# A decoder layer with 32 experts: the final sums, the norm and the output of most tokens moved into the expert loop

## The chip, the cores and the metric

The kernel runs on one core of one Trainium2 chip. The metric is the device time of one execution in microseconds (us), the median of several runs. The engines are TensorE (PE in the profile, its weight loads PEld), VectorE (DVE), ScalarE (ACT), GpSimd (POOL) and SyncE (SP, which here only issues transfers). Each engine works through its own instructions in order and waits on semaphores for the others; a wait holds everything behind it on that engine.

## The reference

One layer on 1024 tokens of 1024 numbers, all float32. Attention comes first, then a mixture of experts:

```
x = x + g1 * sb_mixer(norm(x) * (1 + sc1) + sh1)         # stick-breaking attention, 16 heads
h = norm(x) * (1 + sc2) + sh2
grp = argmax(h @ w_grp + b_grp)                          # 1 of 4 groups of 8 experts
p, top2 = top_k(softmax(expert logits in that group), 2)
y = sum over the 2 experts of gate_e * (silu(h @ w_gate[e]) * (h @ w_up[e])) @ w_down[e]
out = rms_norm(x + g2 * y, final_g)                      # over the 1024 numbers of a token
```

Each token goes to two of the 32 experts, both in the same group. Its output needs both expert results.

## The kernel before

The first 700 us are projections, attention and routing. They leave in DRAM `x1_d` (x after attention) and `h2_d` (the input of the experts), and on the chip, for every expert, a list of its tokens.

The expert loop (from 700 to 1280 us) walks the 32 experts in order, 128 token slots each. A planner's list MU sets the order: four units `gu` (gate and up products, a quarter of the contraction each) of expert e, then two units `dn` (the down product) of expert e - 1. Each unit takes two weight tiles of 512 KB, which SP loads far ahead (as far as the free buffers allow, less a reserve of RM). Matmuls are done in three float32r products of a high and a low part, so every weight tile is split: ACT rounds it to `hi` (L124), DVE subtracts to get `lo` (L127). `m_split(n + SLEAD)` puts the split two units ahead of its use, so in the program ACT and DVE do unit n + 2 right after PE's matmuls of unit n.

Around the units, per expert: POOL gathers the tokens' rows `xg` by an indirect DMA (L1112); PE transposes them (L1140), ACT and DVE split them (`xTh` L1142, `xTl` L1143); after the gate and up products (PE, L1156, L1158, L1160) ACT does Silu and DVE the product `sg` (L1168, L1169); PE transposes `sg` (L1177), ACT and DVE split it (`hhl`, L1181, L1182); after the down product (PE, L1197) DVE multiplies by the gate and by g2 (`ys`, L1209), and POOL scatters `ys` to `y2_d` by an indirect DMA (L1119). `y2_d` has a row per token and choice.

In expert 2, `overflow_lists` counts on DVE whether an expert has more than 128 tokens (L1217 to L1240); PE gives it one small matmul (L1215).

After the loop comes a branch for such overflows (none is taken with these inputs), and then the tail: for each of 8 tiles of 128 tokens SP loads two rows of `y2_d` per token, DVE adds both to x1 (L1370, L1371), ACT sums the squares (L1373), POOL takes the power -1/2 (L1377), DVE scales (L1383), and ACT's queue writes the tile out (L1384).

## Time and profile before

| | us |
|---|---|
| median of 3 runs | 1331.52 (1331.03 to 1332.09) |
| the profiled execution | 1330.46 |
| its span, from the first to the last instruction | 1328.7 |
| PE busy in the span | 1225.2 (92%) |
| DVE busy | 1139.9 (86%) |
| ACT busy | 815.4 (61%) |
| POOL busy | 252.3 (19%) |
| expert loop, per expert (transposes of sg, 1243.3 to 1261.3) | 17.9 |
| from the end of the last matmul to the end of the span | 48.3 |

Busy shares are averages over the whole span. Matmuls overlap each other, and their ends are modelled, so a PE that is busy all the time may still be waiting for its inputs now and then; the start times of its instructions tell. An idle time in brackets is that of the engine before the instruction, with what ended it.

### The profile page before, as it was taken

Reading aid. Unit: us, or ns where it says so; the run is one execution under the profiler, and the core shown is the slowest. Engines: PE = TensorE matmul, PEld = TensorE weight load, DVE = VectorE, ACT = ScalarE, POOL = GpSimd, SP = SyncE. Lnnn points to the kernel's source line nnn. Section 1 sums busy time; section 2 is a strip of 40 time slices with the busy share of each in tenths; the row PEclk is TensorE's granted clock in tenths of the full one; section 3 lists DMA queues with packets and bytes.
Section 4 is the critical chain, followed back from the end, with each engine's and each line's share of the span. In section 5 each row is a group of like instructions: output and inputs, shape, how many; then the busy total and the mean of one; then the engine's idle time right before and its main releaser. Section 6 shows DMA issues by size and latency. Waiting matters only on the chain.

```text
span 1328.7 us, 19369 instructions
## 1 busy us (share of the span) xinstructions
PE 1225.2 (92%) x6788; PEld 983.1 (74%) x6788; DVE 1139.9 (86%) x1518; ACT 815.4 (61%) x1176; POOL 252.3 (19%) x329
## 2 busy tenths in 40 slices
PE   3999999999999999899979999999999999999950
PEld 3887777777777876578867788888888888888830
DVE  5868888988776859958788999999999999999957
ACT  6546455544556657732227778777777877777732
POOL 2502222211122213201211231111111111111101
PEclk9999999999999999999989999999999999999985
DMA  9311234333310212376428999999999999999467
GB/s 358 123 33 40 80 96 135 90 96 99 114 42 25 62 40 87 128 257 235 146 96 342 408 388 386 383 384 384 391 379 391 381 385 375 386 380 391 172 270 274
DMA packets 123395, 306.68 MB, mean 231 GB/s; under 512 B 16976, under 2 KB 49816, under 8 KB 123296
## 3 DMA queue, kind: packets, MB, share of 16 engines
q1 hardware_dynamic: 110256, 275.99, 56.4%
q0 software_dynamic: 11776, 25.20, 5.2%
q10 hardware_dynamic: 1264, 4.23, 0.8%
q8 instruction: 54, 0.88, 0.3%
q14 instruction: 45, 0.37, 0.1%
HBM read 288.58 MB, written 33.57 MB: 242 GB/s over the span
## 4 chain that ended last, share of the span: by engine, by line
issue 45%; PE 33%; DVE 9%; POOL 9%; DMA 2%; ACT 2%; POOLq 0%; SPq 0%; DVEq 0%; ACTq 0%
PE pm L115 6%; PE pm L117 5%; PE pm L116 5%; POOL y_d L1119 5%; PE pm L582 3%; PE z L513 3%; DVE S L540 3%; PE pm L555 3%; POOL xg L1112 2%; PE z L115 2%; PE z L117 2%; PE z L116 2%; DVE lo L127 1%; PE pm L718 1%; DVE p L541 1%
## 5 line engine op out<-in xcount | busy, mean ns | idle before, releaser
L127 DVE TENSOR_TENSOR lo<-wr,hi 128x1024 fp32r<-128x1024 f32 x384 | 447.3, 1221 | 11.5 <-ACT hi L124 7.4
L124 ACT CAST hi<-wr 128x1024 fp32r<-128x1024 f32 x384 | 380.4, 1050 | 17.1 <-PE pm L1197 7.2
L540 DVE TENSOR_TENSOR_SCAN S<-S 128x128 f32<-128x128 f32 (+3 forms) x192 | 186.4, 1012 | 23.1 <-POOL S L522 20.2
L1156 PE MATMUL z<-hi,xTh 128*128 128x512 f32 x512 | 162.2, 398 | 0.8 <-ACT xTh L1142 0.8
L1158 PE MATMUL z<-lo,xTh 128*128 128x512 f32 x512 | 160.3, 393 | 1.1 <-DVE lo L127 0.9
L1160 PE MATMUL z<-hi,xTl 128*128 128x512 f32 x512 | 158.9, 391 | 0.1
L1197 PE MATMUL pm<-hi,hhl 128*128 128x512 f32 x512 | 150.8, 397 | 0.0
L556 ACT COPY aT<-pm 128x512 f32<-128x512 f32 (+2 forms) x192 | 80.8, 493 | 69.3 <-PE pm L555 68.5
L1158 PEld LDWEIGHTS z<-lo,xTh 128*128 128x128 f32 x512 | 96.4, 188 | 23.9 <-DVE lo L127 2.7
L1160 PEld LDWEIGHTS z<-hi,xTl 128*128 128x128 f32 x512 | 96.2, 188 | 21.8 <-DVE xTl L1143 0.4
L520 POOL TENSOR_SCALAR_AFFINE_SELECT S<-S 128x256 f32<-128x256 f32 x64 | 51.1, 799 | 317.7 <-ACT S L516 310.7
L1156 PEld LDWEIGHTS z<-hi,xTh 128*128 128x128 f32 x512 | 93.9, 189 | 19.6 <-ACT xTh L1142 1.2
L1197 PEld LDWEIGHTS pm<-hi,hhl 128*128 128x128 f32 x512 | 94.1, 189 | 18.6
L115 PE MATMUL pm<-hTh,hi 128*128 128x512 f32 x256 | 107.1, 418 | 0.0
L541 DVE TENSOR_TENSOR p<-p,S 128x256 f32<-128x256 f32 (+3 forms) x96 | 92.5, 963 | 10.6 <-ACT p L517 2.0
L516 ACT ACTIVATE S<-z 128x256 f32<-128x256 f32 (+3 forms) x96 | 79.2, 825 | 34.6 <-PE z L513 18.0
L116 PE MATMUL pm<-hTl,hi 128*128 128x512 f32 x256 | 100.2, 392 | 0.0
L117 PE MATMUL pm<-hTh,lo 128*128 128x512 f32 x256 | 100.2, 391 | 0.0
L1119 POOL DMA_INDIRECT y_d<-ys,tbsi x32 | 64.2, 2007 | 188.4 <-DVE ys L1209 184.8
L1112 POOL DMA_INDIRECT xg<-h_d,tbgi x32 | 34.2, 1068 | 305.8 <-PE pm L1140 297.0
L517 ACT ACTIVATE p<-z 128x256 f32<-128x256 f32 (+3 forms) x96 | 78.5, 818 | 22.1 <-DVE acc L461 9.3
L555 PE MATMUL pm<-ident,p 128*128 128x128 f32 x576 | 79.8, 280 | 11.5 <-DVE v L397 6.0
(224 smaller groups left out, 2203.6 us busy)
## 6 DMA issues: line engine op xcount, KB each, us to landing
wr<-in_moe_w_gate_dram SPq DMA_DIRECT2D x128, 512.0 KB, 11.5
wr<-in_moe_w_up_dram SPq DMA_DIRECT2D x128, 512.0 KB, 11.3
wr<-in_moe_w_down_dram SPq DMA_DIRECT2D x128, 512.0 KB, 11.4
ad<-in_ada_w_dram SPq DMA_DIRECT2D x32, 512.0 KB, 4.0
ada<-in_ada_w_dram SPq DMA_DIRECT2D x16, 512.0 KB, 9.0
wq<-in_sb_w_in_dram SPq DMA_DIRECT2D x16, 512.0 KB, 5.1
x<-in_x_dram SPq DMA_DIRECT2D x8, 512.0 KB, 9.3
wv<-in_sb_w_in_dram SPq DMA_DIRECT2D x8, 512.0 KB, 5.4
```

Of the source, the lines that this page charges most:

```text
L115: nc.tensor.matmul(pt, lh, rh, start=start, stop=False)
L116: nc.tensor.matmul(pt, lh, rl, start=False, stop=False)
L117: nc.tensor.matmul(pt, ll, rh, start=False, stop=stop)
L124: nc.scalar.copy(hi, raw)
L127: (nc.vector if lo_eng == "v" else nc.gpsimd).tensor_tensor(lo, raw, hi, op=ALU.subtract)
L540: nc.vector.tensor_tensor_scan(r, r, r, s[:, h, n:n + 1], op0=ALU.mult, op1=ALU.bypass)
L555: nc.tensor.transpose(pt[:, j, :], p[:, h, j * P:(j + 1) * P], ident)
L1119: s = nc.gpsimd.indirect_dma_start(out=y2_d[:, :], out_offset=bass.IndirectOffsetOnAxis(ap=idx, axis=0), in_=ys[:, :], in_offset=None, bou ...
L1156: nc.tensor.matmul(gu[:, s, :], xh_[:, k, :], sp[s][0][:, k2, :], start=k == 0, stop=False)
L1158: nc.tensor.matmul(gu[:, s, :], xh_[:, k, :], sp[s][1][:, k2, :], start=False, stop=False)
L1160: nc.tensor.matmul(gu[:, s, :], xl_[:, k, :], sp[s][0][:, k2, :], start=False, stop=k == ND - 1)
L1197: nc.tensor.matmul(py[nh], a[:, f, :], sp[j][b][:, ns], start=f == 0 and a is hth and b == 0, stop=f == NF - 1 and a is htl)
```

## The change

Tokens are put in the order of the later one of their two experts. The first 128 tokens of that order are expected to be done after expert 8, the next after 12, and so on (`DONE`); seven of the eight tiles of 128 get their sum, norm and output inside the loop or right behind it, and the eighth after the branches.

- In routing, `r_gate` also keeps the later expert of each token (`later`).
- In expert 2, behind the overflow lists, `order_tokens` computes each token's place in that order: eight small additions in a row on DVE, three small matmuls on PE, and more DVE work. Then POOL writes the token numbers to `perm_d` by eight indirect DMAs of 128 numbers each, loads the list back as `permc`, and DVE makes `perm2` from it and tests on the chip whether the first seven tiles are really done at their experts (`bad`, counted into `ctl`).
- Two experts after `DONE`, POOL gathers the tile's rows of x1 and both of `y2_d`. One expert later DVE adds, scales by g2 and adds (`f_sum` in three steps, one behind each of the first three splits), ACT sums the squares, POOL takes the power, DVE scales, and POOL scatters the rows to the output.
- The product with g2 leaves `y_unit`: it becomes one ACT instruction per half with the gate as scale.
- `y2_d` is filled with zeros in the attention stage (four writes of 2 MB), because a tile is gathered while later experts are missing if the test fails.
- If the test fails, a second branch does the seven tiles once more. The reserve RM is 7 in place of 4.

The diff, cut to its core:

```
-RM = 4
+RM = 7
+DONE = (8, 12, 16, 20, 24, 28, 30)
...
+    perm_d = dram.tile([T, 1], I32, name="perm_d")
...
+        nc.vector.tensor_tensor(later[:, t:t + 1], ef[:, 0:1], ef[:, 1:2], op=ALU.max)
...
+            if hp == 5 and u in (0, 2, 4, 6):
+                if u == 0:
+                    yz = blk(nm="yz")
+                    nc.gpsimd.memset(yz, 0.0)
+                nc.sync.dma_start(y2_d[u * 256:u * 256 + 512, :].rearrange("(a p) d -> p a d", p=P),
+                                  yz[:, None, :].to_broadcast([P, 4, 1024]))
...
-            nc.vector.scalar_tensor_tensor(ys[:, ns], py[nh], gate[:, e:e + 1], g2r[:, ns], op0=ALU.mult, op1=ALU.mult)
+            nc.scalar.activation(ys[:, ns], py[nh], AF.Copy, scale=gate[:, e:e + 1])
...
+        bad, many = order_tokens(thr), small([P, 1], nm="many", bufs=1, pool=more)
+        nc.vector.tensor_reduce(many, bad, axis=AX, op=ALU.add)
+        nc.vector.tensor_tensor(ctl[:, 17:18], many, cum[:, 31:32], op=ALU.add)
...
+    def order_tokens(thr):
+        lastm = blk((P, NT, 32), BF16, nm="lastm")
+        nc.vector.tensor_tensor(lastm, io128[:, None, 0:32].to_broadcast([P, NT, 32]),
+                                later[:, :, None].to_broadcast([P, NT, 32]), op=ALU.is_equal)
+        lastc = blk((P, NT + 1, 32), BF16, nm="lastc")
+        nc.vector.memset(lastc[:, 0, :], 0.0)
+        for t in range(NT):
+            nc.vector.tensor_tensor(lastc[:, t + 1, :], lastc[:, t, :], lastm[:, t, :], op=ALU.add)
...
+        nc.tensor.matmul(pr[:, 0:256], tri, lastm.rearrange("p t e -> p (t e)"), start=True, stop=False)
+        nc.tensor.matmul(pr[:, 0:256], onesb, lastc[:, 0:NT, :].rearrange("p t e -> p (t e)"), start=False, stop=True)
+        nc.tensor.matmul(pc[:, 0:32], onesb, lastc[:, NT, :], start=True, stop=True)
...
+        nc.vector.tensor_copy(spi, spf)
+        ws = []
+        for t in range(NT):
+            w = nc.gpsimd.indirect_dma_start(out=perm_d[:, :],
+                                             out_offset=bass.IndirectOffsetOnAxis(ap=spi[:, t:t + 1], axis=0),
+                                             in_=tokc[:, t:t + 1], in_offset=None, bounds_check=T - 1,
+                                             oob_is_err=False)
...
+        nc.gpsimd.dma_start(permc, perm_d.rearrange("(s p) o -> p (s o)", p=P))
+        nc.vector.tensor_scalar(perm2, permc, float(T), None, op0=ALU.add)
+        bad = small([P, 7], nm="bad", bufs=1, pool=more)
+        nc.vector.tensor_tensor(bad[:, 0:6], cum[:, 8:29:4], thr[:, 0:6], op=ALU.is_lt)
+        nc.vector.tensor_tensor(bad[:, 6:7], cum[:, 30:31], thr[:, 6:7], op=ALU.is_lt)
...
+    def f_gather(s, c1, c2):
+        FX[s] += [blk(nm="fa"), blk(nm="fb")]
+        rows_of(FX[s][1], y2_d, c1, 2 * T)
+        rows_of(FX[s][2], y2_d, c2, 2 * T)
+
+    def f_sum(s, step):
+        fx, fa, fb = FX[s]
+        if step == 0:
+            nc.vector.tensor_tensor(fa, fa, fb, op=ALU.add)
+        elif step == 1:
+            nc.vector.tensor_tensor(fa, fa, g2r, op=ALU.mult)
+        else:
+            nc.vector.tensor_tensor(fx, fx, fa, op=ALU.add)
+            nc.scalar.activation(fb, fx, AF.Square, accum_out=ss)
+            nc.scalar.activation(ms, ss, AF.Identity, scale=1.0 / D, bias=epsc)
+            nc.gpsimd.tensor_tensor(rstd, ms, mhalf, op=ALU.pow)
+
+    def f_out(s, c1):
+        fx, rstd = FX.pop(s)
+        nc.vector.scalar_tensor_tensor(fx, fx, rstd, fgr, op0=ALU.mult, op1=ALU.mult)
+        nc.gpsimd.indirect_dma_start(out=out[0], out_offset=bass.IndirectOffsetOnAxis(ap=c1, axis=0),
+                                     in_=fx[:, :], in_offset=None, bounds_check=T - 1, oob_is_err=False)
...
             m_split(n + SLEAD)
+            for s_, d_ in enumerate(DONE[:6]):
+                if e == d_ + 2 and q == 0:
+                    f_rows(s_, col(permc, s_))
+                    f_gather(s_, col(permc, s_), col(perm2, s_))
+                if e == d_ + 3 and q < 3:
+                    f_sum(s_, q)
+            if e == E - 1 and q == 3:
+                for s_ in (6, 7):
+                    f_rows(s_, col(permc, s_))
...
             m_split(n + SLEAD)
             m_fill(RM, len(MU))
+            for s_, d_ in enumerate(DONE[:6]):
+                if e == d_ + 2 and q == 0:
+                    f_out(s_, col(permc, s_))
...
                 y_unit(e)
+                if e == DONE[6]:
+                    f_gather(6, col(permc, 6), col(perm2, 6))
+    for k in range(3):
+        f_sum(6, k)
+    f_out(6, col(permc, 6))
     nx = nc.values_load(ctl[0:1, 16:17], min_val=0, max_val=15)
+    again = nc.values_load(ctl[0:1, 17:18], min_val=0, max_val=32)
...
-    for t in range(4):
-        f_load(t)
-    for t in range(NT + 1):
-        if t < NT:
-            f_sum(t)
-            if t + 4 < NT:
-                f_load(t + 4)
-        if t > 0:
-            f_out(t - 1)
+    with tc.If(again > 0):
+        with tc.For_i(0, 7, 1) as j:
+...
+    f_gather(7, col(permc, 7), col(perm2, 7))
+    for k in range(3):
+        f_sum(7, k)
+    f_out(7, col(permc, 7))
```

What it moves on the engines is seen best in their instruction order. First DVE in expert 2, at the end of the overflow lists and the start of the splits for expert 3 (`ctl` holds the overflow counts, `wr` is a raw weight tile). Before:

```order
L1236 TENSOR_TENSOR xb_7644<-io_312,xb_7644 128x16 [waits DVE_49]
L1237 TENSOR_SCALAR xb_7644<-xb_7644 128x16 [waits DVE_49]
L1239 TENSOR_SCALAR ctl_7648<-xe_7641 128x16
L1240 CAST ctl_7648<-cum_7637 128x1
L127 TENSOR_TENSOR lo_7667<-wr_7238,hi_7666 128x1024 [waits DMAHW4_49,Activation_49]
L127 TENSOR_TENSOR lo_7671<-wr_7240,hi_7670 128x1024 [waits DMAHW5_49,Activation_49]
```

And in the changed kernel, whose line numbers are its own (`spi` are the places that POOL's eight writes go to, `permc` the list that it loads back):

```order
L1291 TENSOR_REDUCE spf_7688<-sp_7685 128x8 [waits DVE_49]
L1294 CAST spi_7690<-spf_7688 128x8 [waits DVE_49]
L1306 TENSOR_SCALAR perm_7117<-permc_7116 128x8 [waits DMASW7_49]
L1308 TENSOR_TENSOR bad_7718<-lcum_7682,thr_7641 128x6
L1309 TENSOR_TENSOR bad_7718<-lcum_7682,thr_7641 128x1
L1257 TENSOR_REDUCE many_7721<-bad_7718 128x1 [waits DVE_49]
L1258 TENSOR_TENSOR ctl_7658<-many_7721,cum_7647 128x1 [waits DVE_49]
L128 TENSOR_TENSOR lo_7740<-wr_7276,hi_7739 128x1024 [waits DMAHW0_49,Activation_49]
L128 TENSOR_TENSOR lo_7744<-wr_7278,hi_7743 128x1024 [waits DMAHW1_49,Activation_49]
```

The splits now stand behind an instruction that waits for a DMA of POOL's (DMASW7).

Second, ACT in an expert that carries a tile (expert 11, from its second `gu` unit on). Before:

```order
L1181 CAST hhl_9232<-pm_9227 128x512 [waits PE_49]
L124 CAST hi_9247<-wr_8859 128x1024 [waits DMAHW4_49,DVE_49]
L124 CAST hi_9251<-wr_8861 128x1024 [waits DMAHW5_49,DVE_49]
L124 CAST hi_9271<-wr_8891 128x1024 [waits DMAHW6_49,PE_49]
L124 CAST hi_9275<-wr_8893 128x1024 [waits DMAHW7_49,PE_49]
L1168 ACTIVATE sg_9283<-z_9178 128x512 [waits PE_49]
```

And in the changed kernel (`fx` is the tile's sum, which DVE's third step of `f_sum` writes):

```order
L1195 CAST hhl_9317<-pm_9312 128x512 [waits DVE_49,PE_49]
L125 CAST hi_9332<-wr_8990 128x1024 [waits DMAHW1_49]
L125 CAST hi_9336<-wr_8992 128x1024 [waits DMAHW2_49]
L1338 ACTIVATE fb_9097,ss_9341<-fx_9092 128x1024 [waits DMASW2_49,DVE_49]
L1340 ACTIVATE fms_9343<-ss_9341,epsc 128x1 [waits Activation_49]
L125 CAST hi_9367<-wr_9019 128x1024 [waits DMAHW3_49,PE_49]
L125 CAST hi_9371<-wr_9021 128x1024 [waits DMAHW4_49,PE_49]
L1182 ACTIVATE sg_9379<-z_9257 128x512 [waits PE_49]
```

Two casts of `hi` now stand behind a sum of squares that waits for DVE.

Third, POOL at the end of the loop. Before it has only the last scatters and the branch:

```order
L1119 DMA y_d<-ys_7651,tbsi_7105 2048x1024 [waits DMASW5_49,DVE_49]
L1119 DMA y_d<-ys_7444,tbsi_7105 2048x1024 [waits DMASW6_49,DVE_49]
L1119 DMA y_d<-ys_7651,tbsi_7105 2048x1024 [waits DMASW7_49,DVE_49]
L1294 TENSOR_LOAD ctl_7648 [waits DMAHW3_49,DMAHW2_49,DMAHW4_49,DMAHW1_49,DMAHW5_49,DMAHW0_49,DMAHW6_49,DVE_49,DMAHW7_49,Activation_49,Pool_49]
L1295 COMPARE_AND_BRANCH
```

And in the changed kernel:

```order
L1133 DMA y_d<-ys_7458,tbsi_7122 2048x1024 [waits Activation_49]
L1316 DMA fa_13169<-y_d,permc_7116 128x1024 [waits DMASW2_49,DMASW1_49,PE_49]
L1316 DMA fb_13170<-y_d,perm_7117 128x1024 [waits PE_49]
L1133 DMA y_d<-ys_7724,tbsi_7122 2048x1024 [waits DMASW3_49,DMASW2_49,Activation_49]
L1342 TENSOR_TENSOR frstd_13215<-fms_13213,mhalf 128x1 [waits Activation_49]
L1349 DMA out_dram<-fx_13099,permc_7116 1024x1024 [waits DMASW5_49,DMASW0_49,DVE_49]
L1419 TENSOR_LOAD ctl_7658 [waits DMAHW3_49,DMAHW2_49,DMAHW4_49,DMAHW1_49,DMAHW5_49,DMAHW0_49,DMAHW6_49,DVE_49,DMAHW7_49,Activation_49,Pool_49]
L1420 TENSOR_LOAD ctl_7658 [waits DVE_49]
L1421 COMPARE_AND_BRANCH
```

The gathers of tile 6 stand ahead of the last expert's scatter, which waits for both of them (DMASW2, DMASW3), and tile 6's output stands ahead of the branches.

## Rows read from the trace of the kernel before

**Rows 1.** Busy time by stretch; columns: stretch, length, engines, PE clock, DMA share, GB/s

```profile
700.00:704.00 4.00, 3.89 (x14) 3.34 (x15) 4.00 (x16) 2.49 (x4) 0.99 (x1) 0.56 0.32 111
705.00:770.00 65.00, 63.03 (x291) 50.72 (x291) 61.13 (x70) 48.34 (x56) 10.21 (x7) 1.00 1.02 406
850.00:1150.00 300.00, 300.00 (x1408) 249.12 (x1407) 294.19 (x302) 232.75 (x270) 45.04 (x33) 1.00 1.00 383
```

**Rows 2.** Waits for the split, 770 to 1250 us: who, for whom, total, times, longest

```profile
ACT hi L124 <- PE pm L1197: 7.2, 26, 0.3
DVE lo L127 <- ACT hi L124: 5.0, 24, 0.3
```

**Rows 3.** Timeline of DVE in expert 2: start, us, engine, line, operation

```profile
746.86 0.39 DVE L1222 TENSOR_TENSOR gtb<-cnts,thr 128x224 f32<-128x224 f32 x1
...
751.27 0.15 DVE L1240 CAST ctl<-cum 128x1 int32<-128x1 f32 x1
751.33 2.35 DVE L127 TENSOR_TENSOR lo<-wr,hi 128x1024 fp32r<-128x1024 f32 x2
```

**Rows 4.** Timeline of PE in expert 2

```profile
745.13 0.19 PE L1215 MATMUL pm<-macc,onesb 128*128 128x32 bf16 x1
...
752.60 0.49 PE L1158 MATMUL z<-lo,xTh 128*128 128x512 f32 x1 [0.25 <-DVE lo L127]
```

**Rows 5.** Timeline of POOL: the first and the third of three gathers issued in a row

```profile
695.73 1.10 POOL L1112 DMA_INDIRECT xg<-h_d,tbgi  x1 [5.62 <-DVE e L837]
...
698.46 1.34 POOL L1112 DMA_INDIRECT xg<-h_d,tbgi  x1 [0.30 <-issue]
```

**Rows 6.** The gathers of xg between 694 and 704 us (4 of them)

```profile
DMA to landing us min/median/max: 4.2/4.6/5.4
```

**Rows 7.** The gathers of xg between 770 and 1230 us (25 of them)

```profile
DMA to landing us min/median/max: 7.2/7.4/8.7
```

**Rows 8.** POOL's writes of x1_d (512 KB each, 600 to 700 us)

```profile
DMA to landing us min/median/max: 2.9/3.6/7.0
```

**Rows 9.** POOL's writes of mod_d (2 KB each)

```profile
DMA to landing us min/median/max: 1.6/1.8/6.2
```

**Rows 10.** Timeline of DVE in experts 29 and 30

```profile
1239.09 1.40 DVE L1209 SCALAR_TENSOR_TENSOR ys<-pm,tbl,g2r 128x512 f32<-128x512 f32 x2
1240.41 4.62 DVE L127 TENSOR_TENSOR lo<-wr,hi 128x1024 fp32r<-128x1024 f32 x4
```

**Rows 11.** Timeline of ACT there

```profile
1236.67 4.85 ACT L124 CAST hi<-wr 128x1024 fp32r<-128x1024 f32 x5
```

**Rows 12.** Timeline of PE there: readings of lo by three units, and the last matmuls

```profile
1253.46 0.63 PE L1197 MATMUL pm<-lo,hhl 128*128 128x512 f32 x2
...
1256.20 0.62 PE L1158 MATMUL z<-lo,xTh 128*128 128x512 f32 x2
...
1262.16 0.63 PE L1158 MATMUL z<-lo,xTh 128*128 128x512 f32 x2
...
1279.84 0.61 PE L1197 MATMUL pm<-hi,hhl 128*128 128x512 f32 x2
```

**Rows 13.** Timeline of DVE in the tail

```profile
1288.91 1.22 DVE L1370 TENSOR_TENSOR ya<-ya,x 128x1024 f32<-128x1024 f32 x1 [7.23 <-DMA ya<-y_d]
...
1295.43 1.28 DVE L1383 SCALAR_TENSOR_TENSOR x<-x,frstd,fgr 128x1024 f32<-128x1024 f32 x1 [0.47 <-POOL frstd L1377]
```

**Rows 14.** Timeline of ACT in the tail

```profile
1295.04 1.06 ACT L1373 ACTIVATE yb<-x 128x1024 f32<-128x1024 f32 x1 [0.72 <-DVE x L1371]
```

**Rows 15.** Timeline of POOL in the tail

```profile
1281.95 0.97 POOL L1119 DMA_INDIRECT y_d<-ys,tbsi  x1 [3.66 <-DVEq L1295]
...
1296.60 0.55 POOL L1377 TENSOR_TENSOR frstd<-fms,mhalf 128x1 f32<-128x1 f32 x1 [1.20 <-ACT fms L1375]
```

**Rows 16.** SP's first load, and ACT's last two writes, of the tail

```profile
1285.29 0.33 SPq L1363 DMA_DIRECT2D ya<-y_d  x1
...
1319.77 2.53 ACTq L1384 DMA_DIRECT2D out_dram<-x  x2
```

More of the change, by code (lines that the diff above doesn't have):

```diff
@@ L683, in decoder_layer @@
     mcum = [macc0]
+    later = const.tile([P, NT], F32, name="later")
     posall = const.tile([P, 2 * NT], F32, name="posall")
@@ L1237, in overflow_lists @@
         nc.vector.tensor_scalar(xb, xb, 1.0, float(P), op0=ALU.add, op1=ALU.mult)
-        ctl = small([P, 17], I32, nm="ctl", bufs=1, pool=more)
+        ctl = small([P, 18], I32, nm="ctl", bufs=1, pool=more)
         nc.vector.tensor_scalar(ctl[:, 0:16], xe, 31.0, None, op0=ALU.min)
@@ L1241, in overflow_lists @@
         free(gtb, le)
+        bad, many = order_tokens(thr), small([P, 1], nm="many", bufs=1, pool=more)
+        nc.vector.tensor_reduce(many, bad, axis=AX, op=ALU.add)
+        nc.vector.tensor_tensor(ctl[:, 17:18], many, cum[:, 31:32], op=ALU.add)
         return ctl, xb
+    permc = small([P, NT], I32, nm="permc", bufs=1, pool=more)
+    perm2 = small([P, NT], I32, nm="perm2", bufs=1, pool=more)
+    def order_tokens(thr):
[6 more added lines that the diff above has]
+            nc.vector.tensor_tensor(lastc[:, t + 1, :], lastc[:, t, :], lastm[:, t, :], op=ALU.add)
+        tokc = blk((P, NT), I32, nm="tokc")
+        nc.gpsimd.iota(tokc, pattern=[[P, NT]], base=0, channel_multiplier=1)
+        pr, pc = pm(), pm()
+        nc.tensor.matmul(pr[:, 0:256], tri, lastm.rearrange("p t e -> p (t e)"), start=True, stop=False)
+        nc.tensor.matmul(pr[:, 0:256], onesb, lastc[:, 0:NT, :].rearrange("p t e -> p (t e)"), start=False, stop=True)
+        nc.tensor.matmul(pc[:, 0:32], onesb, lastc[:, NT, :], start=True, stop=True)
+        tot = small([P, 32], nm="ltot", bufs=1, pool=more)
+        nc.vector.tensor_copy(tot, pc[:, 0:32])
+        cum = small([P, 32], nm="lcum", bufs=1, pool=more)
+        nc.vector.tensor_tensor_scan(cum, tot, tot, 0.0, op0=ALU.add, op1=ALU.bypass)
+        nc.vector.tensor_tensor(tot, cum, tot, op=ALU.subtract)
+        a = blk((P, NT, 32), nm="sp")
+        nc.vector.tensor_tensor(a, pr[:, 0:256].rearrange("p (t e) -> p t e", e=32),
+                                tot[:, None, :].to_broadcast([P, NT, 32]), op=ALU.add)
+        free(pr, pc)
+        nc.vector.tensor_tensor(a, a, lastm, op=ALU.mult)
+        spf = small([P, NT], nm="spf", bufs=1, pool=more)
+        nc.vector.tensor_reduce(spf, a, axis=AX, op=ALU.add)
+        free(a, lastm, lastc)
+        spi = small([P, NT], I32, nm="spi", bufs=1, pool=more)
+        nc.vector.tensor_copy(spi, spf)
[5 more added lines that the diff above has]
+                                             oob_is_err=False)
+            for o in ws:
+                tc.declare_no_dep(w.ins, o.ins, reason="each token has a place of its own")
+            ws.append(w)
+        free(tokc)
+        nc.gpsimd.dma_start(permc, perm_d.rearrange("(s p) o -> p (s o)", p=P))
[3 more added lines that the diff above has]
+        nc.vector.tensor_tensor(bad[:, 6:7], cum[:, 30:31], thr[:, 6:7], op=ALU.is_lt)
+        return bad
@@ new lines, in decoder_layer, with rows_of, f_rows @@
+    FX = {}
+    def rows_of(dst, src, idx, n):
+        nc.gpsimd.indirect_dma_start(out=dst[:, :], out_offset=None, in_=src[:, :],
+                                     in_offset=bass.IndirectOffsetOnAxis(ap=idx, axis=0),
+                                     bounds_check=n - 1, oob_is_err=False)
+    def f_rows(s, c1):
+        FX[s] = [blk(nm="fx")]
+        rows_of(FX[s][0], x1_d, c1, T)
+    def f_gather(s, c1, c2):
+        FX[s] += [blk(nm="fa"), blk(nm="fb")]
+        rows_of(FX[s][1], y2_d, c1, 2 * T)
+        rows_of(FX[s][2], y2_d, c2, 2 * T)
@@ new lines, in f_sum @@
+    def f_sum(s, step):
[6 more added lines that the diff above has]
+            nc.vector.tensor_tensor(fx, fx, fa, op=ALU.add)
+            ss = small([P, 1], nm="ss", bufs=3, pool=more)
+            nc.scalar.activation(fb, fx, AF.Square, accum_out=ss)
+            ms = small([P, 1], nm="fms", bufs=3, pool=more)
+            nc.scalar.activation(ms, ss, AF.Identity, scale=1.0 / D, bias=epsc)
+            rstd = small([P, 1], nm="frstd", bufs=3, pool=more)
+            nc.gpsimd.tensor_tensor(rstd, ms, mhalf, op=ALU.pow)
+            free(fa, fb)
+            FX[s] = (fx, rstd)
```

52 lines of the change are left out of this document (19 added, 33 removed).

## The prediction

> **What bounds the kernel now.** I read the busy times by stretch first, then the waits, then the timelines of the three places where the order changes. Between 850 and 1150 us PE is busy for 300.00 of 300 us at its full clock, DVE for 294.19, ACT for 232.75, and the DMA engines are at share 1.00 with 383 GB/s [rows 1]. A busy PE alone proves little, so the waits decide: no row there has PE waiting for anything, and no split waits for a load; the splits wait 7.2 us for PE and 5.0 us for ACT in 480 us [rows 2]. So PE's own pace bounds the loop, at 17.9 us an expert. DVE has about 2% in hand, which the departing `ys` widens by 1.40 us an expert [rows 10]. That removal cannot speed the loop up; what the change can win is in the tail, 48 us without a matmul, and it pays for that by what it puts into the loop.
>
> DVE's lead over PE is short. The program splits two units ahead, 6.0 us by PE's readings of `lo` at 1256.20 and 1262.16 [rows 12], and a unit's two splits take 2.3 of that (four in 4.62 [rows 10]). A DVE that stands still for longer than the rest stops PE.
>
> **Expert 2: the order of tokens.** Here lies the largest term. Today DVE ends the overflow lists at 751.42 and starts the splits for expert 3 at 751.33 [rows 3]; the first of them is what PE waits for at 752.60 [rows 4], so every later start there is PE's delay. Now between the two:
>
> - The test for equality (256 numbers, as the 0.39 us of 224 [rows 3], so 0.43), a small memset (0.15), eight additions at about 0.21 with their gaps (the small cast takes 0.15 [rows 3]): 753.7. PE's three small matmuls at 0.19 [rows 4] wait for that: 754.3. Copy, scan, subtraction, three passes over 256 numbers and a cast, 2.3: the places are ready at 756.6.
> - POOL issues eight indirect DMAs. Three in a row start 1.36 us apart [rows 5], so the eighth starts at 756.7 + 7 x 1.36 = 766.2. It lands 4.6 us later when the queues are nearly empty [rows 6], 7.4 when they are full [rows 7]. No buffer comes free while DVE stands, so loads cease: I take 4.6, 770.8.
> - POOL loads the list. Its plain writes land after 3.6 us [rows 8], so at 774.6. It can't be less than 1.6 (2 KB, [rows 9]).
> - DVE makes `perm2` and four small results, 5 x 0.21: 775.7.
>
> The splits start 24.4 us late. Of that PE can fill nothing: what it has in hand (two `dn` units, 6.6 us) it would have done anyway. The clock adds to it: around 700 us, after short waits, PE ran at 0.56 of its clock for 4 us [rows 1], 1.2 GHz for most of them, so I add 1.7: 26.1. Bounds: both landings at 1.6 and issues at 0.97 apart [rows 15] give 16; issues 2 us apart and both landings at 8.7 [rows 7] give 38.
>
> The Trainium skill, DMA: Bandwidth & Descriptors, section "Anatomy of one DMA — SWDGE (gpsimd) path", gives a DMA of POOL about 2.0 us fixed plus its bytes at 436 GB/s. For 512 KB that is 3.2; the gathers here take 4.2 at the least [rows 6], so the trace disagrees. By the rule both landings would be 2.0 and this term, as an estimate from that page, 22 us.
>
> **Six tiles inside the loop.** Each adds to one expert on DVE three sums of 1.22 and a scaling of 1.28 [rows 13], 4.9 us, and on ACT a sum of squares of 1.06 that waits for the third sum. I walked it in the clock of expert 30 [rows 10 to 12], with DVE's splits 1.14 apart.
>
> - `ys` on ACT waits for PE's last `dn` matmul and takes 1.1 us at 1237.8 in front of a pair of casts, which thus end at 1240.8 and not 1239.6. DVE, rid of `ys`, ends that pair at 1242.25 (1242.7 before): nothing lost, and nothing in an expert without a tile.
> - First sum to 1243.4, next pair 1245.65, second sum 1246.8, `hhl`, next pair 1249.65, third sum 1250.8. The sum of squares and its two small followers take 1.56 [rows 14, 15]: 1252.35. Only now come ACT's next casts, and DVE's first split behind them ends at 1254.6. PE wants it at 1253.46 [rows 12]: 1.1 late.
> - The next two pairs, with `sg`, the scaling and `xTl` between, end at 1258.55 and 1263.25, wanted at 1256.4 and 1259.2: 1.05 and 1.9 more. Then DVE is ahead again.
>
> That is 4.0 us a tile, 20 for five. The sixth falls into expert 31, where PE waits for `sg` anyway and `sg` is behind the whole walk: 5.5. Together 25.5. Below, a tile may hide altogether but for the excess of DVE's work over its slack (4.9 - 1.4 - 0.4 - 2 of lead, 1 us each: 6); above, late gathers and the clock falling in each stall (1.7 each) give 45.
>
> The gathers themselves I cost at nothing: from a scatter one expert earlier (1239.5 - 17.9 = 1221.6) its landing (8.7, as the slowest gather [rows 7]) and two gathers (1.4 + 8.7) end at 1240.4, and the first sum comes at 1242.25. The DMA traffic too: six times 2.1 MB. The queues carried 406 GB/s from 705 to 770 us against 383 needed [rows 1]; in the 71 us between tiles that is room for 1.6 MB, and the rest comes to about 1 us a tile, for which the loads run ahead.
>
> **The tail.** In the clock of before, with PE's end at 1280.45 [rows 12]. The scatter of expert 30 issues two `dn` units (5.5) before the last, 1276.5, and lands 3.2 later (1281.95 to 1285.2 [rows 15, 16]), 1279.7; tile 6's gathers start 1.36 apart behind it and land 4.6 later, 1285.9; the last scatter waits for them and for nothing else, 1286.1 in place of 1281.95, but this is not what ends last. Tile 6: sums to 1289.5, squares 1291.05, power 1292.2, scaling 1293.5, POOL's scatter 1294.6. Behind it on POOL stand two branches at about 2 us (scatter issued at 1282.92, first load past the branch at 1285.29 [rows 15, 16]): 1298.8. Tile 7: gathers landed 1304.9, sums 1308.5, scaled 1312.5, issue. Today from the last write's issue (about 1322) to the end of the span are 6.7 us [rows 16]; I take 8 for the scatter: 1320.5, against 1328.7. Gain 8 (2 to 13). Seven tiles out of eight buy so little because a chain of DMA, sums, power, DMA is now passed twice in a row on POOL.
>
> **The rest.** Zero writes and one memset in the attention stage, one small maximum per routing tile, behind a PE that is bound by itself: 0.5 (0 to 4). With RM at 7 two units less are loaded ahead; no split waits for a load today [rows 2], so nothing.
>
> **Sum.** 1330.46 + 26.1 + 25.5 - 8 + 0.5 = 1374.6. The median of the runs is 1.1 above the profiled execution: 1376. Own range 1360 to 1392.
>
> **Rivals.**
>
> - The tiles hide nearly all, the order costs as worked out: 1330.5 + 26.1 + 6 - 8 + 0.5 + 1.1 = 1356. For it speaks that ACT has 22% idle time and DVE gains 1.4 us an expert; against it that a sum of squares in ACT's order waits for DVE. 0.19.
> - The DMA engines become the bound, at 383 GB/s whatever is asked: 12.6 MB more is 33 us, of which the loads' lead swallows a share that no row here shows; between 0 and 33 I take 19: 1376 + 19 = 1395. For it: share 1.00 [rows 1]. Against: 406 GB/s for 65 us. 0.08.
> - The other side: DVE's wait for the list is short, since the eight writes overlap with the overflow lists' work or land at once, and the sums fit into DVE's slack. Then only the tail counts: 1331.5 - 8 + 2 = 1325, down to 1319. It decides at a wait of about 6 us, the tail's gain; the issue of eight DMAs alone takes 9.5. 0.09, of it 0.02 within 0.2%.
> - The test on the chip fails, and seven tiles are done again at about 20 us each (the steps of tile 7): 1516. Counted from the reference's inputs, 259, 361, 570, 654, 776, 839 and 940 tokens are done where 128 to 896 are asked. 0.02.
>
> My forecast keeps 0.62. What a measurement of this kernel can tell from no change is about 0.2%. Slower: 0.62 + 0.19 + 0.08 + 0.02 = 0.91; within 0.2%: 0.02; faster: 0.07. The range from 1342 to 1404 holds the first two rivals and leaves out the last two and the bounds' corners.
>
> **What would show it.** In expert 2 DVE idles for 15 us or more in front of L1306, with a DMA as what ended it, and PE for about as long behind it. In each expert with a tile ACT waits for DVE in front of L1338, and PE's `lo` matmuls wait for DVE. POOL's last scatter waits for tile 6's gathers. From the end of the last matmul to the end of the span it is about 40 us and not 48. I am wrong if DVE's wait in expert 2 is under 8 us, or if PE never waits in the experts with tiles.

## The result, and the profile after

The changed kernel takes 1412.42 us (median of 4 runs, 1409.21 to 1413.72) against 1331.37 us for the kernel before beside it: a ratio of 1.0603, 95% interval 1.059 to 1.0615. The forecast was 1376, with 1404 as its upper end. The direction was right, the size was not: 81 us are lost where 44.5 were expected. The profiled execution of the changed kernel has a span of 1411.8 us, 83.1 more than before.

Where the 83 us lie is read from PE: an expert's length is taken from its first `lo` matmul (L1158 before, L1172 now) to that of the next expert, and each stage is compared with the same stage of the kernel before.

| stage | forecast, us | measured, us |
|---|---|---|
| up to the first expert | 0.5 (the rest) | +2.3 |
| experts 2 and 3 (order of tokens) | +26.1 | +25.7 |
| the experts with a tile's sums: 11, 15, 19, 23, 27 | +20 for these two rows | +8.3 |
| the experts behind them: 12, 16, 20, 24, 28 | | +48.9 |
| expert 31 (sixth tile of sums) | +5.5 | +7.9 |
| all other experts | 0 | +0.2 |
| end of the last matmul to the end of the span | -8 | -10.2 (48.3 to 38.1) |

One row holds nearly the whole error: the expert *behind* the one with the sums.

The waits of the changed kernel from 700 to 1360 us: who waited for what, us in total, times, longest.

```profile
ACT hi L125 <- issue: 38.7, 5, 8.3
...
ACT fb L1338 <- DVE fx L1336: 27.0, 6, 4.5
...
DVE perm L1306 <- DMA permc<-perm_d: 19.4, 1, 19.4
PE z L1172 <- DVE lo L128: 18.8, 12, 14.1
...
PE z L1170 <- ACT hi L125: 14.4, 10, 3.9
...
PE pm L1191 <- DVE sg L1183: 7.0, 1, 7.0
```

In [rows 2] PE waited for nothing. Three of the rows here were forecast: DVE's wait for the list, ACT's squares waiting for DVE, PE waiting for `sg` in expert 31. The first was not: ACT stands five times before a cast, 8.3 us at the longest, "issue" being the profile's word for a wait whose end it can't name. The timeline in expert 12 names it (all engines; start, us, engine, line, operation, and in brackets the idle time before it):

```profile
947.40 1.28 ACT L1223 ACTIVATE ys<-pm,tbl 128x512 f32<-128x512 f32 x2
...
948.07 1.03 POOL L1349 DMA_INDIRECT out_dram<-fx,permc  x1 [7.02 <-DVE fx L1348]
...
956.09 1.99 ACT L125 CAST hi<-wr 128x1024 fp32r<-128x1024 f32 x2 [7.41 <-issue]
957.17 1.23 DVE L128 TENSOR_TENSOR lo<-wr,hi 128x1024 fp32r<-128x1024 f32 x1 [5.92 <-ACT hi L125]
...
957.19 0.50 PE L1170 MATMUL z<-hi,xTh 128*128 128x512 f32 x1 [1.87 <-ACT hi L125]
```

And the scatters of finished rows between 940 and 960 us:

```profile
L1349 POOL DMA_INDIRECT out_dram<-fx,permc x1: 1026/1026/1026, 948.1 to 948.1; - x1
...
DMA to landing us min/median/max: 8.0/8.0/8.0
```

948.07 + 8.0 = 956.1: the cast starts when the tile's output has landed. `f_out` hands `fx` back to the list of free blocks right behind the scatter that still reads it; the list is first in, first out, and holds eight other blocks at that point, so the next expert's new `hi` is put into that very block while the scatter reads it. The program's order had it in plain sight: from expert 4 on just five casts of `hi` name a queue of POOL's (DMASW), one for each tile. Here is the one of the first tile, with ACT's rows around it:

```
L1223 ACTIVATE ys_7458<-pm_9383,tbl 128x512 [waits PE_49]
L125 CAST hi_9473<-wr_9156 128x1024 [waits DMAHW1_49,DMASW5_49,DVE_49]
L125 CAST hi_9477<-wr_9158 128x1024 [waits DMAHW2_49]
```

Expert 2 went almost as worked out. Timelines of POOL, DVE and PE there, where DVE and PE went on without a pause before [rows 3, 4]:

```profile
758.68 1.02 POOL L1297 DMA_INDIRECT perm_d<-tokc,spi  x1 [11.67 <-DVE spi L1294]
...
767.73 0.98 POOL L1297 DMA_INDIRECT perm_d<-tokc,spi  x1 [0.30 <-issue]
774.31 0.97 POOL L1305 DMA_DIRECT2D permc<-perm_d  x1 [5.60 <-DMA perm_d<-tokc,spi]
...
777.28 0.17 DVE L1306 TENSOR_SCALAR perm<-permc 128x8 int32<-128x8 int32 x1 [19.39 <-DMA permc<-perm_d]
...
777.90 2.36 DVE L128 TENSOR_TENSOR lo<-wr,hi 128x1024 fp32r<-128x1024 f32 x2
...
779.18 0.79 PE L1172 MATMUL z<-lo,xTh 128*128 128x512 f32 x1 [14.06 <-DVE lo L128]
```

Expert 2 begins 1.9 us later here than before. Less that, the places are ready at 756.0 (forecast 756.6), the eighth transfer is issued at 765.8 (766.2), the eight have landed at 772.1 (770.8), the list is back at 775.3 (774.6), and the splits start at 776.0 (775.7). The stretches by engine, with PE's granted clock (columns as in [rows 1]; the last two rows belong to the stall in expert 12):

```profile
747.30:753.70 6.40, 0.00 (x0) 0.00 (x0) 6.00 (x16) 2.56 (x3) 0.00 (x0) 0.74 1.03 408
753.70:765.10 11.40, 10.28 (x37) 7.68 (x36) 3.44 (x15) 3.55 (x5) 4.95 (x5) 0.69 0.90 358
765.10:779.20 14.10, 0.04 (x2) 0.03 (x1) 1.85 (x7) 0.72 (x3) 5.98 (x6) 0.59 0.48 100
779.20:784.60 5.40, 5.05 (x11) 3.46 (x12) 5.40 (x6) 3.94 (x4) 0.00 (x0) 0.50 0.26 93
...
955.30:957.20 1.90, 0.03 (x2) 0.01 (x1) 0.03 (x1) 1.11 (x2) 0.00 (x0) 1.00 1.03 395
957.20:962.10 4.90, 3.96 (x9) 2.58 (x10) 4.90 (x5) 4.90 (x6) 0.00 (x0) 0.65 0.71 268
```

PE's idle time comes in two pieces, which the forecast had not told apart: 6.4 us in front of the three small matmuls, which stand ahead of the `dn` units in PE's order and wait for DVE's additions, and 14.1 us behind those units. Behind each the granted clock is lower (0.69 and 0.50), and behind the 1.9 us in expert 12 too (0.65 of full speed, that is 1.2 GHz for most of the 4.9 us): each of these three stalls costs PE more than its idle time.

The tail, POOL's timeline (before, [rows 15, 16]):

```profile
1375.00 1.02 POOL L1316 DMA_INDIRECT fb<-y_d,perm  x1 [0.30 <-issue]
1381.00 1.40 POOL L1133 DMA_INDIRECT y_d<-ys,tbsi  x1 [4.98 <-DMA fb<-y_d,perm]
...
1392.26 1.03 POOL L1316 DMA_INDIRECT fa<-y_d,permc  x1 [3.37 <-issue]
...
1406.56 1.04 POOL L1349 DMA_INDIRECT out_dram<-fx,permc  x1 [1.61 <-DVE fx L1348]
```

The last expert's scatter waits for tile 6's gathers, and the chain from gather to scatter is passed twice, as forecast.

### The profile page after: what moved, and what is told of

It is laid out like the page before. It is cut to its first block, busy times and chain, and to the rows that moved or that the text cites. A ratio compares the mean times of both kernels' runs of the same rounds, so it can differ in the third digit from the quotient of the medians.

```text
span 1411.8 us, 19435 instructions
## 1 busy us (share of the span) xinstructions
PE 1263.6 (90%) x6791; PEld 1000.5 (71%) x6791; DVE 1116.5 (79%) x1492; ACT 847.9 (60%) x1240; POOL 277.3 (20%) x372
## 5 line engine op out<-in xcount | busy, mean ns | idle before, releaser
L1172 PE MATMUL z<-lo,xTh 128*128 128x512 f32 x512 | 170.0, 410 | 18.8 <-DVE lo L128 18.8
L1170 PE MATMUL z<-hi,xTh 128*128 128x512 f32 x512 | 170.8, 414 | 14.6 <-ACT hi L125 14.4
L1174 PE MATMUL z<-hi,xTl 128*128 128x512 f32 x512 | 166.7, 408 | 6.5 <-DVE xTl L1157 6.5
L1211 PE MATMUL pm<-hi,hhl 128*128 128x512 f32 x512 | 154.1, 404 | 1.5 <-ACT hi L125 1.5
L1172 PEld LDWEIGHTS z<-lo,xTh 128*128 128x128 f32 x512 | 100.4, 196 | 47.6 <-DVE lo L128 24.9
L1170 PEld LDWEIGHTS z<-hi,xTh 128*128 128x128 f32 x512 | 98.0, 197 | 39.9 <-ACT hi L125 17.3
L1174 PEld LDWEIGHTS z<-hi,xTl 128*128 128x128 f32 x512 | 100.2, 197 | 30.7 <-DVE xTl L1157 8.4
L1126 POOL DMA_INDIRECT xg<-h_d,tbgi x32 | 41.6, 1299 | 280.9 <-PE pm L1154 254.8
L1211 PE MATMUL pm<-lo,hhl 128*128 128x512 f32 x256 | 82.2, 403 | 2.6 <-DVE lo L128 2.6
```

The source lines that it names most:

```text
L1170: nc.tensor.matmul(gu[:, s, :], xh_[:, k, :], sp[s][0][:, k2, :], start=k == 0, stop=False)
L1172: nc.tensor.matmul(gu[:, s, :], xh_[:, k, :], sp[s][1][:, k2, :], start=False, stop=False)
L1174: nc.tensor.matmul(gu[:, s, :], xl_[:, k, :], sp[s][0][:, k2, :], start=False, stop=k == ND - 1)
L1211: nc.tensor.matmul(py[nh], a[:, f, :], sp[j][b][:, ns], start=f == 0 and a is hth and b == 0, stop=f == NF - 1 and a is htl)
```

## The experiments

All medians are of runs beside the kernel before on the same chip; ratios are to it. The stages below are differences from the profiled execution of the kernel before, read as in the table above ("sums" and "next" are the five experts with a tile's sums and the five behind them in the changed kernel). They are read from one profiled execution of each run, which lies up to 5 us from the run's median (e3's 8 us above it), so a row does not add up to the median beside it.

| run | us | ratio (95%) | start | experts 2, 3 | sums | next | expert 31 | tail, whole |
|---|---|---|---|---|---|---|---|---|
| after | 1412.4 | 1.060 (1.059 to 1.062) | +2.3 | +25.7 | +8.3 | +48.9 | +7.9 | 38.1 |
| e1 | 1384.4 | 1.039 (1.037 to 1.041) | +2.8 | +25.9 | +8.2 | +16.6 | +6.9 | 38.2 |
| e2 | 1408.9 | 1.058 (1.056 to 1.060) | +2.6 | +21.0 | +8.3 | +44.3 | +7.3 | 38.4 |
| e3 | 1416.5 | 1.062 (1.060 to 1.064) | +3.3 | +27.8 | +17.6 | +47.0 | +8.5 | 38.1 |
| e4 | 1386.0 | 1.040 (1.039 to 1.042) | -0.1 | +19.0 | +16.9 | +19.1 | +8.5 | 38.3 |
| e5 | 1396.3 | 1.047 (1.044 to 1.051) | +2.4 | +8.3 | +8.3 | +49.2 | +8.3 | 38.0 |
| e6 | 1363.5 | 1.024 (1.022 to 1.026) | +0.4 | +26.3 | +0.2 | +10.2 | +4.3 | 38.2 |
| e7 | 1360.0 | 1.021 (1.019 to 1.023) | +0.8 | +25.7 | +0.1 | +0.6 | +8.4 | 38.2 |
| e8 | 1338.5 | 1.005 (1.003 to 1.006) | +3.2 | -0.3 | +11.1 | +3.2 | +10.6 | 31.0 |
| e9 | 1335.9 | 1.003 (1.002 to 1.004) | +3.8 | -0.3 | +6.2 | +1.4 | -0.1 | 46.3 |
| e10 | 1337.7 | 1.004 (1.003 to 1.006) | +0.3 | 0.0 | -0.3 | +0.5 | +2.4 | 51.1 |
| e11 | 1331.0 | 0.999 (0.998 to 1.000) | +2.7 | 0.0 | -0.3 | +0.5 | +5.4 | 40.5 |
| e12 | 1325.6 | 0.995 (0.994 to 0.997) | +3.2 | 0.0 | -0.3 | +0.5 | 0.0 | 41.3 |

**e1, the block held back.**

```
-        free(fx)
+        if s in range(6):
+            FX[s] = fx          # freed in the fourth expert after DONE
```

> The changed kernel with one edit: the block of a tile's sum, fx, goes back to the free list one expert later than its output scatter, not right behind it. Theory: in the second expert of each of five tiles ACT's cast writes the new hi into the block that the scatter is still reading, and stands 8.3 us or so until the scatter has landed; PE loses 9.0 to 10.8 us there, 49.9 us in five. With the block held back those go, less what DVE's lag costs there instead (0 to 2.5 us each): 1412 - 50 + 0 to 12 = 1362 to 1375, and no wait of ACT's cast with a landing scatter behind it. Rival: the stall is what DVE's and ACT's extra work or crowded transfers cost (the forecast's own reasons), and the scatter's landing only falls together with it: 1400 or more.

Measured: 1384.4, 28 us less. The five casts no longer stand (no row of ACT's `hi` waiting for "issue" is left), and "next" falls from 48.9 to 16.6. The theory of the block holds, and the rival (1400 or more) is out. The total is still above the theory's 1362 to 1375: 3.3 us an expert are left in "next", where 0 to 2.5 were allowed. So 24.8 us in ten experts stay, 5.0 a tile. That is close to the 4.0 that the forecast had for the squares: the long stall had covered them. In expert 11 and 12 (ACT and DVE):

```profile
939.33 1.06 ACT L1338 ACTIVATE fb<-fx 128x1024 f32<-128x1024 f32 x1 [4.45 <-DVE fx L1336]
...
940.72 1.98 ACT L125 CAST hi<-wr 128x1024 fp32r<-128x1024 f32 x2
...
941.78 2.36 DVE L128 TENSOR_TENSOR lo<-wr,hi 128x1024 fp32r<-128x1024 f32 x2 [2.48 <-ACT hi L125]
```

**e2, the list awaited later; e5, with its source block held back too.**

```
+                if e == 5:      # perm2, bad and many, before: in expert 2
+                    bad, many = order_check(thr, lcum), small([P, 1], nm="many", bufs=1, pool=more)
...                              # e5 only:
-        free(tokc)
+        TOK.append(tokc)        # freed in order_check
```

> The changed kernel with one edit: perm2 and the test on the chip are worked out behind expert 5, so DVE doesn't wait in expert 2 for the list to come back. Theory: of the 25.7 us that PE loses from expert 2 to expert 3, the 19.4 us that DVE waits go; what stays is DVE's own work on the order (about 5 us) and PE's three matmuls that stand ahead of the down product and wait for it, with the clock at half behind that: 6 to 9 us stay, 1412 - 18 = 1394 (1390 to 1398). Rival: PE's idle time in front of the three matmuls (6.4 us) and the eight transfers are what costs, the wait only lies over it: 1400 to 1408.

> The run with perm2 and the test behind expert 5, and one more edit: the block of the token numbers, tokc, which POOL's eight writes read, also goes back to the free list there. Theory: with perm2 moved alone, DVE's xTl of expert 4 was put into that block and waited 14.7 us for the eight writes to land, so one wait for a transfer took the place of the other. With the block held back expert 2 and 3 together take 28.7 + 20.5 us instead of 64.2: 1412 - 15 = 1397 (1394 to 1400) in the terms of the changed kernel; some 10 us stay, PE's 6.4 us in front of the three small matmuls and the clock at half behind them. Rival: POOL, held by the landing of the eight writes, passes its lateness on through the gathers and scatters queued behind: 1403 to 1409.

e2 missed: 1408.9, only 3.5 us less. One row of its waits (745 to 800 us) says why:

```profile
DVE xTl L1157 <- DMA perm_d<-tokc,spi: 14.7, 1, 14.7
```

The same fault once more: `tokc`, which the eight transfers read, had been freed, and `xTl` was put into its block. e5 holds it back: 1396.3, and experts 2 and 3 lose 8.3 us and no longer 25.7. What stays is the piece in front of the small matmuls.

```profile
PE pm L1276 <- DVE lastc L1270: 6.4, 1, 6.4
```

So of the 25.7 us, 17.4 were the wait for the list and 8.3 PE's wait for DVE's additions, with the clock (6.4 of it idle).

**e3 and e4, a failed try at the squares.** Both were to put the squares one unit later (e4 with e1's and e2's edits). As edited they also add the third sum twice, so their output is not that of the layer, and DVE has 1.2 us more of work for each tile.

```
-        else:
+        else:                   # now also for step 3
             nc.vector.tensor_tensor(fx, fx, fa, op=ALU.add)
+        if step == 3 or step == 2 and s not in range(6):
```

> The changed kernel with one edit: the sum of squares of a tile stands one unit later in ACT's order, behind the next pair of casts, so that it needn't wait for DVE's third sum with casts behind it. Theory: each of five tiles loses 1.5 to 1.8 us in the expert of its sums, and that is ACT's wait for DVE in front of the squares; it goes, but the wait for the output scatter stays and takes part of it back: 1412 - 8 + 0 to 6 = 1404 to 1410. Rival (the forecast as put): the squares' place is worth 4 us a tile, 20 in all: 1392. Second rival: DVE's extra work alone makes the lag: 1411 to 1413.

> The changed kernel with the three edits together (block of fx held back an expert, perm2 and the test behind expert 5, squares a unit later). Theory: the causes lie in different places, so the gains add up: 1412 - 44 - 18 - 8 = 1342 (1334 to 1350), which is the kernel before (1331) plus some 9 us in expert 2, some 8 in the last expert, 3 to 8 for DVE's work on the tiles, less 10 in the tail. Rival: DVE's 4.9 us of extra work a tile are the real bound and what is removed comes back as waits of PE for lo: 1365 or more.

Both came out above what was expected (1416.5 and 1386.0), and neither decides on the squares, since each changes their place and DVE's work at once. The expert of the sums loses 3.5 and 3.4 us a tile, where it lost 1.7 before the edit. That more work on DVE at this place is paid for would fit, but isn't shown by them. In e4 the wait of `xTl` for the eight transfers stands as in e2 (13.5 us).

**e6, e1 with the squares a unit later; e7, e1 with a tile's DVE steps on four experts (the sixth tile's are spread over expert 31).**

```
-        else:
+        elif step == 2:
             nc.vector.tensor_tensor(fx, fx, fa, op=ALU.add)
+        else:                   # squares, Identity, power
...                              # e6:
-                if e == d_ + 3 and q < 3:
+                if e == d_ + 3:
...                              # e7:
+                    if e in (d_ + 3, d_ + 4, d_ + 5) and q == 0:
+                        f_sum(s_, e - d_ - 3)
+                    if e == d_ + 6 and q == 0:
+                        f_out(s_, col(permc, s_))
```

> The run with fx's block held back, and the sum of squares one unit later in ACT's order, behind the casts of the next unit (the earlier try at this also added the third sum twice, which this one doesn't). Theory: in that run (1384) a tile still costs 4.2 to 5.6 us; DVE stands for 2.5 us behind the squares in ACT's order, the rest is its own 4.9 us. Without the 2.5 us in five tiles: 1384 - 12 = 1372 (1366 to 1376). Rival: DVE's work alone sets it and the 2.5 us were slack: 1381 to 1386.

> The run with fx's block held back, and a tile's four steps of DVE on four experts in a row, one step each; the squares a unit behind the third sum; the sixth tile's steps (its two experts are the last) at the first and third unit of expert 31, behind the last split, and behind the last unit. Theory: DVE gains 1.4 us an expert from the moved gate product and has some 0.4 in hand; one step of 1.22 to 1.28 an expert fits, so five tiles cost next to nothing and the sixth 2 to 4 instead of 7: 1384 - 21 - 4 = 1359 (1354 to 1365). Rival: the 4.9 us have no room however they lie (DVE is busy for 98% of the loop): 1372 to 1382.

e6 gains more than expected (1363.5): of 5.0 us a tile the squares' place was 2.9, and 2.1 are DVE's own work on top of its splits. Some 5 us of the gain lie elsewhere, 2.6 in expert 31 and 2.4 in the start, which the edit doesn't touch. In e7 the 2.1 us go too. Five tiles in the loop cost 0.7 us together, and DVE's 4.9 us a tile have room if they come one step an expert. e7's total (1360.0) is as expected, but partly by luck: the five tiles gave 24 us and not 21, and expert 31, where 4 us were to be won, loses 8.4, more than in e1. From 850 to 1250 us of e7 (columns as in [rows 1]):

```profile
850.00:1250.00 400.00, 400.00 (x1874) 331.70 (x1873) 381.68 (x376) 338.46 (x417) 88.35 (x68) 1.00 1.00 386
```

PE is busy all the time, but so are the DMA engines, at 386 GB/s.

**e8, e7 with the order in six pieces from expert 3 to 7 and two tiles behind the branches; e9, three tiles in the loop.**

```
+ORDAT = ((3, 0), (3, 1), (3, 3), (4, 2), (5, 0), (7, 0))
...
+            if (e, q) in ORDAT:
+                next(ordr, None)
...
+    for s in (6, 7):
+        f_gather(s, col(permc, s), col(perm2, s))
...                              # e9:
-            for s_, d_ in enumerate(DONE[:6]):
+            for s_, d_ in enumerate(DONE[:3]):
```

> The run with the steps on four experts, and two more parts: the order of the tokens as six pieces from expert 3 to 7, none of which waits for a transfer of its own (tokc held back); and two tiles, not one, behind the branches, with the four gathers in a row, so that the chain from gather to scatter is passed once and not twice. Theory: expert 2 gives back 25, the tail 8 to 10 more: 1359 - 25 - 9 = 1325 (1318 to 1333), at the kernel before or a little under it. Rival: the 5 us of DVE's work on the order and two tiles' sums behind the last matmul eat the gain, or another block is waited for: 1338 or more.

> The run with everything (1339), but three tiles in the loop and five behind the branches, all ten gathers there in a row and a tile's scale behind the next tile's sums. Theory: in the run with everything no engine's work stops PE any more but casts wait for loads from expert 11 on; each tile moves 2.1 MB, 5.4 us at 385 GB/s, and the list's single numbers cost the queues another 9 us, against some 20 us by which loads land ahead; six tiles (42 us) use that up, 14 us are lost. Three tiles (16 + 9) nearly fit: 0 to 5 us of waits for loads; the tail costs 3.7 us for each tile more, 31 + 11 = 42. So 1339 - 10 to 14 - 10 (expert 31, which carries no tile now) + 11 = 1328 (1324 to 1332). Rival: the waits for loads come with any tile in the loop and don't depend on how many have gone before: half of the 14 stays, 1335 or more.

e8 missed (1338.5 for 1325). Expert 2 costs nothing any more and the tail is 7 us shorter, and yet it is 0.5% slower than the kernel before. 14.3 us come back in the experts with tiles, now as waits for loads (840 to 1250 us; in e7 such rows come to 1.1 us, in the kernel before there is none):

```profile
ACT hi L126 <- DMA wr<-in_moe_w_up_dram: 19.9, 25, 2.2
ACT hi L126 <- DMA wr<-in_moe_w_down_dram: 18.8, 33, 1.4
...
ACT hi L126 <- DMA wr<-in_moe_w_gate_dram: 9.1, 11, 2.3
```

And by stretch:

```profile
800.00:850.00 50.00, 50.00 (x235) 41.49 (x234) 46.64 (x50) 41.97 (x52) 17.12 (x15) 1.00 0.99 319
850.00:900.00 50.00, 50.00 (x236) 41.29 (x235) 46.32 (x47) 40.64 (x50) 9.85 (x8) 1.00 1.01 388
...
850.00:1250.00 400.00, 392.76 (x1807) 318.26 (x1806) 371.38 (x363) 328.57 (x400) 93.31 (x65) 1.00 1.00 387
```

The last row is the stretch shown for e7: 387 GB/s and there 386, but PE is idle for 7.2 us in it, and has 1807 matmuls where e7 has 1874.

How far ahead a load lands of the cast that reads it tells the rest (worked out from the landing of a weight load and the start of its cast, for the half of the loads whose landing the trace gives; medians by expert). Before it is 18 to 19 us in every expert from 3 to 20. In e7, whose 25 us stall in expert 2 lets the loads run on, it is 26 in expert 10 and falls by some 5 a tile to 1 in expert 27. In e8 it is 19 in expert 6, 6 in expert 8, 2 from expert 11 to 14 and nothing from 15 on. So the forecast's rival of the DMA engines was the next bound, hidden by the stalls in front of it. And e8 lost most of its lead before any tile was gathered: in the 50 us from 800 on, where the list's single numbers are written (issued from 799 to 810 us), the queues move 319 GB/s at a share of 0.99, against 388 in the 50 us behind.

e9 fits this in kind but misses in size (1335.9 for 1328): 7.6 us are still lost in the experts with tiles, and five tiles need a tail of 46 and not 42. The number is that of its rival (half of the 14 stays, 1335 or more), but not the reason: the loss grows with the tiles that have gone before, 0 us in experts 11 and 12, 1.9 in 15 and 16, 5.1 in 19 and 20, and 0.2 at most in an expert behind the last of the three.

**e10, all sums at the end; e11, without waits between rows that differ; e12, gathers later.** The order is kept (nine pieces, expert 3 to 18), but no sum is in the loop; `ys` is DVE's again, with g2, and the reserve RM is 4 again. Six tiles are gathered in experts 29 and 30, two behind the first branch; the redoing branch stands last.

```
+            if e in (29, 30) and q < 3:
+                s_ = 3 * (e - 29) + q
+                f_rows(s_, col(permc, s_))
+                f_gather(s_, col(permc, s_), col(perm2, s_))
...                              # e11:
+                for o in scat[DONE[s] + 1:]:
+                    tc.declare_no_dep(g.ins, o.ins, reason="rows of later experts; if the test fails they are done again")
...                              # e12:
-            if e in (29, 30) and q < 3:
+            if e in (29, 31) and q < 3:
...
+    for k in range(4):           # ahead of the last two tiles' gathers
+        f_sum(1, k)
```

> The order of the tokens kept (nine pieces from expert 3 to 18), but no sum in the loop: the gate product as in the kernel before (VectorE, with g2), six tiles gathered in experts 29 and 30, when the last weights are on their way, the other two behind the first branch, all sums from the last splits on, and the branch that redoes tiles at the very end. Theory: in the kernel before DVE stands from 1277 to 1289 us with only one ys to do, until rows have landed behind the branch; with rows there early eight tiles at 3.7 us and one ys run from 1277 to 1308, and the end is some 6 us behind: 1314, with up to 2 more for the start of the loop: 1317 (1311 to 1324). Rival: the gathers in experts 29 and 30 take the loads' lead (9.5 MB, 25 us, against 22) and stop PE there, or POOL's row of transfers (33 at 1.3 us) becomes the bound: 1326 or more.

> The run with all sums at the end (1338), with one edit: the six early tiles' gathers and the scatters of experts later than DONE (and later gathers and earlier scatters) no longer wait for each other; their rows differ where the test on the chip holds, and are gathered again where it doesn't. Theory: in that run the scatter of expert 29 waited for gathers until 1287 us, ys of expert 31 for that scatter's buffer (DVE stood 8.9 us), and the squares' power for POOL's row behind it (7.1 us); with the waits gone DVE runs from 1277 almost without a stop, 30 us of tiles and 1.4 of ys, 1309, and the end comes 6 us later: 1316 (1311 to 1323). Rival: POOL's row itself (33 transfers at 1.3 us, some at 2) is the bound and only moves the wait: 1328 or more.

> The last run (1331) with two edits: three of the six early tiles are gathered in expert 31 and not in expert 30, and the second tile's sums, squares and power stand ahead of the last two tiles' gathers. Theory: in that run casts in expert 31 waited for loads (expert 31 took 29.6 us and not 24.3, PE stood 4.1 us for sg), since six tiles' gathers (9.4 MB) ran beside the last weights; three less take that away or most of it; and DVE stood 4.1 us for a power that POOL did only behind four gathers. 1331 - 4 - 4 = 1323 (1318 to 1328). Rival: the gathers are only late in their turn and hold the tail by what they save: 1329 to 1333.

e10 missed (1337.7 for 1317). The loop is as before, but DVE stands where it was to work:

```profile
1280.20 1.23 DVE L1340 TENSOR_TENSOR fx<-fx,fa 128x1024 f32<-128x1024 f32 x1
1290.30 1.41 DVE L1224 SCALAR_TENSOR_TENSOR ys<-pm,tbl,g2r 128x512 f32<-128x512 f32 x2 [8.87 <-DMA y_d<-ys,tbsi]
```

The `ys` of expert 31 waits for the scatter of expert 29 to release its buffer, and that scatter stood behind the gathers. e11 takes these waits away: 1331.0, level with the kernel before (ratio 0.998 to 1.000), and 15 us short of the 1316: casts in expert 31 now wait for loads (+5.4 us), a power stands behind four gathers on POOL (DVE idles for 4.1 us), and 2.7 us lie in the start. e12 gathers three tiles later and puts that power first: expert 31 is back at its length, and at 1325.6 us (ratio 0.9952, 0.9937 to 0.9966) it beats both kernels, the one before by 0.5%. Expert 31 gave what was gained; the power's wait only moved by a tile:

```profile
1294.79 1.23 DVE L1346 TENSOR_TENSOR fx<-fx,fa 128x1024 f32<-128x1024 f32 x1
1300.17 1.28 DVE L1359 SCALAR_TENSOR_TENSOR fx<-fx,frstd,fgr 128x1024 f32<-128x1024 f32 x1 [4.16 <-POOL frstd L1353]
```

## Why the prediction was right or wrong

- **What bounds the kernel before: right, and half of it.** PE set the pace, but the loads ran level with it. That no split waited for a load [rows 2] showed a lead of 18 to 19 us, not room for more; e8 used it up.
- **Expert 2, 26.1 forecast, 25.7 measured: right**, chain and size. One cause was not priced, PE's 6.4 us in front of the small matmuls. It adds nothing while PE waits for the late splits anyway; e5 separates it. By the Trainium skill, DMA: Bandwidth & Descriptors, section "Anatomy of one DMA — SWDGE (gpsimd) path", the term was an estimate of 22 us; the eight writes took 6.3 us from the last issue to the landing of all, against 2.0 by the rule, so the trace disagrees.
- **Six tiles inside the loop, 25.5 forecast, 65.1 measured: this is the step that failed.** Its walk through expert 30 ended with "Then DVE is ahead again". The walk counted who waits for the new work, and not who takes the block that the new work gives back. The scatter of the finished rows stood in it at nothing; in fact the next expert's cast waits for its landing, 8.0 to 8.8 us after the issue. Of the 39.6 us above the forecast, e1 takes 32.3 back. What the walk did count was sound in kind and near in size: with the block held back the ten experts lose 24.8 us (20 forecast), of which e6 gives 14.4 to the squares' place in ACT's order and e7 the rest to DVE's steps standing together.
- **The sixth tile, 5.5 forecast, 7.9 measured: right in kind.** PE waits for `sg` 7.0 us.
- **The gathers and their traffic at nothing: right for this kernel**, because the stalls kept the loads ahead (by 26 to 35 us from expert 6 on); wrong as soon as they are gone (e8). The queue time of the list's small writes was not priced at all.
- **The tail, a gain of 8 forecast, 10.2 measured: right**, with the wait of the last scatter where it was expected.
- **The start, 0.5 forecast, 2.3 measured: nearly all of it the clock, whose cause stays open.** Up to 568 us the two profiled executions stay within 0.4 us of each other, zero writes included. Then 1.7 us arise around 572.7 to 576.2, where PE's granted clock is 0.53 (before 1.00), and 0.7 in the last routing matmuls (689.6 to 691.6 us, 0.50; before, the same matmuls at 1.00); 0.2 is left for the rest. The waits in front of the first place are nearly the same in both (1.54 and 1.40 us, before 1.47 and 1.40). Over the thirteen kernels with the zero writes the first expert starts -0.1 to +3.8 us from that of the one profiled execution before. Why the clock falls in one and not in the other no run shows.
- **Its signs of being wrong did not show.** DVE waited 19.4 us in expert 2, and ACT and PE waited in the experts with tiles, as it said. They tested the costs that it had counted, not the one that it had left out.
- **The rivals.** The tiles hiding nearly all (1356): e7 shows that five of the six can, in another order. The DMA engines (1395): not here, but next. The other side (1325): reached only by e12, which leaves the loop alone.

## What to carry to other kernels

When a change frees a buffer behind a transfer, look for the next writer of that block and put the transfer's landing into its start; the program's order names the wait, since that instruction waits for a queue it never waited for. A stall also covers what lies behind it: the cost of a change measured with a stall in place is not the sum of its parts, and taking the stall away shows the next bound. Where transfers and the engine run level, as here, what is added to the queues is paid from the lead of the loads (some 5 us for a tile's 2.1 MB), so transfers that can wait belong where the queues have room.
